# Expert weights as unsplit fp32 on 64- and 32-column tiles: experts ranked by size on chip, 1 MB chunks addressed by register

## The chip, the core and the metric

The kernel runs on one core of one Trainium2 chip. The metric is device time in microseconds (us), from the start to the end of one execution. The engines are PE (TensorE, matmuls), PEld (its weight loads), DVE (VectorE), ACT (ScalarE), POOL (GpSimd) and SP (SyncE, which here only issues transfers). All arithmetic that the reference asks for is fp32.

## What is computed

Two model blocks run one after the other on 512 tokens of width 1024. The change lies in the mixture of experts of the first block, which has 32 experts, of which each token uses four. Each expert multiplies its tokens by a 1024x2048 matrix (gate and up), applies a clipped SwiGLU, and multiplies by a 1024x1024 matrix (down).

```python
def moe_ffn(h, router_w, router_b, w_gate_up, b_gate_up, w_down, b_down):
    logits = (hf @ router_w + router_b).astype(jnp.float32)
    top_logits, top_idx = lax.top_k(logits, TOP_K)          # TOP_K = 4, N_EXPERTS = 32
    gates = jax.nn.softmax(top_logits, axis=-1)
    ...
    def expert_block(args):
        xb, e = args
        gu = xb @ w_gate_up[e] + b_gate_up[e]
        gate, up = jnp.split(gu, 2, axis=-1)
        gate = jnp.minimum(gate, SWIGLU_LIMIT)
        up = jnp.clip(up, -SWIGLU_LIMIT, SWIGLU_LIMIT)
        act = (up + 1.0) * gate * jax.nn.sigmoid(SWIGLU_ALPHA * gate)
        return act @ w_down[e] + b_down[e]
    ...
    y_sorted = yb.reshape(n_rows, d)[dest] * gate_sorted[:, None]
    out = jnp.zeros((n, d), h.dtype).at[tok_sorted].add(y_sorted)
```

Ahead of it stand a hybrid mixer and a layer norm, beside it a gated embedding (`ple`), behind it a layer norm and the second block (attention, a recurrent group and an FFN). One expert's weights are 12 MiB (12.58 MB), all 32 are 403 MB. The 512 tokens give 2048 rows, 64 for an expert on average; with the inputs that are timed the largest expert has 95.

## The kernel before

Every fp32 weight is split into two fp32r parts. `Stream` loads pieces of 128x1024 (0.5 MB) on SP's queue (L170), ACT rounds each to `hi` (L187), DVE subtracts to get `lo` (L196), and a product of 512 columns is three fp32r matmuls, `hi`x`hi`, `lo`x`hi`, `hi`x`lo` (`mm3`, L242 to L244). The tokens of an expert are the stationary operand, the weights stream past.

An expert takes up to CAP = 96 tokens, which fill 96 of the 128 columns. For expert e the loop issues `gate_up(e, 0)`, `down(e - 1)`, `gate_up(e, 1)`: two bias matmuls for each half (L976) and 144 matmuls. Between them stand the steps that prepare the expert after next: `find_a` (one-hot rows on DVE, L900), `find_b` (positions by matmul, L910), `find_c`, `gather` (POOL fetches the rows by index), and `turn` (transposes, L934, split again by ACT and DVE). `activate` is the SwiGLU on DVE and ACT, `finish` scales by the gate and POOL adds the rows into `acc` by index (L1034). What is over 96 rows goes to a loop (L1049) that runs as often as a number in `exi` says, here not at all.

The loads of SP stand in the order of use, and each waits for its place to come free: 12 raw places and some that are lent. A gate_up piece has rows of 2 KB in DRAM, a down piece rows of 4 KB. Behind the last expert `load_next` queues the first weights of block 2 (L170), the sums `rest` (L1180) and six rows of norm weights (L1176), and L1211 adds the last two experts' rows into `rest`.

Ahead of the experts stand, in this order on PE, the last of the first `ple` gate, 24 matmuls of `ple_proj`, the counts that give each row its position (L941, L944), and the second `ple` gate in four parts, with `find_b(0)` between.

Of the kernel before, what the change touches and what calls it, by code (L numbers as in the profile page):

```python
# [24 lines left out]
CAP = 96  # L25
# [13 lines left out]
    0, 128, 256, 384, 512, 544, 548, 549, 551, 583)  # L39
NC1 = 615  # L40
# [4 lines left out]
def constants():  # L45
# [5 lines left out]
    c[:, C_SLOT:C_SLOT + 128] = p[None, :]  # L51
# [30 lines left out]
def prepare(i):  # L82
# [27 lines left out]
    o["w_down"] = a["w_down"][0]  # L110
# [15 lines left out]
class Stream:  # L126
# [22 lines left out]
    def lend(self, *places):  # L149

        self.lent += places
        self.loads()

    def _load(self):
        i = self.nl
        ap, shape = self.plan[i]
        if self.lent:
            t = self.taken[i] = self.lent.pop(0)
            self.once.add(i)
        elif self.extra and i < len(self.plan) - self.keep_off:  # L160
# [12 lines left out]
    def loads(self):
        while not self.hold and self.nl < len(self.plan) and (
                self.inring < self.nring or self.lent or self.extra and self.nl < len(self.plan) - self.keep_off):
            self._load()

    def _hi(self):
        i = self.ns
        n, dest = self.units[i]  # L180
        t = self.raw[i]
        if dest is not None:
            hi, lo = dest
        else:
            hi, lo = [t_[:, :n] for t_ in self.hl(self.nh)]
            self.nh += 1
        self.nc.scalar.copy(hi, t)  # L187
        self.parts[i] = (hi, lo)
        self.half = (lo, t, hi)
        self.ns += 1  # L190

    def _lo(self):
        if self.half is not None:
            lo, t, hi = self.half
            self.half = None
            self.nc.vector.tensor_tensor(lo, t, hi, op=ALU.subtract)  # L196
            del self.raw[self.ns - 1]
            slot = self.taken.pop(self.ns - 1, None)
            if slot is None:
                self.inring -= 1  # L200
            elif self.ns - 1 not in self.once:
                self.extra.append(slot)
            self.loads()

# [18 lines left out]

@with_exitstack
def kernel(ctx: ExitStack, tc: tile.TileContext, h, out, dbg=None):
# [7 lines left out]
    psum = ctx.enter_context(tc.tile_pool(name="psum", bufs=1, space=PSUM))  # L233

# [36 lines left out]
    def raw_of(pool, n):  # L271
        return pool.tile([128, 1024], F32, tag="raw", bufs=n, name="raw")

    def parts_of(pool, n):
        return [pool.tile([128, 1024], F32R, tag=g, bufs=n, name=g) for g in ("hi", "lo")]
# [18 lines left out]
    NRING2, NHL2 = 4, 5  # L294
    st2 = Stream(nc, lambda i: raw_of(keep, 4), lambda i: parts_of(keep, 5), NRING2, NHL2)
# [8 lines left out]
    with ExitStack() as first:  # L304
        NRING, NHL = 12, 6
# [6 lines left out]
        selr = btp.tile([128, NE], F32R, name="selr")  # L312
# [3 lines left out]
        st = Stream(nc, lambda i: raw_of(keep, 4) if i % 3 == 0 else raw_of(ring, 8),  # L316
                    lambda i: parts_of(ring, 1) if i % 6 == 5 else parts_of(keep, 5), NRING, NHL)
# [47 lines left out]
        def plan_gu(e, hf):  # L365
            w = h["w_gate_up"][e].rearrange("(k p) c -> p k c", p=128)
            for k in range(2):
                for g in range(2):
                    c0 = 1024 * g + 512 * hf
                    st.add([(w[:, 4 * k:4 * k + 4, c0:c0 + 512], (4, 512))])  # L370

        def plan_d(e):
            w = h["w_down"][e].rearrange("(k p) c -> p k c", p=128)
            for k in range(4):
                st.add([(w[:, 2 * k:2 * k + 2, :], (2, D))])

        for e in range(NE):
            plan_gu(e, 0)
            if 0 < e < NE - 1:
                plan_d(e - 1)  # L380
            plan_gu(e, 1)
        plan_d(NE - 2)
        plan_d(NE - 1)
        st.keep_off = 24
# [341 lines left out]
        bts = slot("y1", [128, D])  # L726
        for r in range(4):
            c0 = 1024 * (r // 2)
            nc.sync.dma_start(bts[32 * r:32 * r + 32], h["b_gate_up"][:, c0:c0 + 1024])

        def split_biases():
            S.copy(btab, bts)
            for r in range(4):
                q = slice(32 * r, 32 * r + 32)
                S.copy(selr[q], ident[q, q])
                if r % 2:
                    tt(btab[q], bts[q], btab[q], op=ALU.subtract)
# [18 lines left out]
        st.extra.append(slot("y2", [128, D]))  # L756
        st.loads()
        ln_b(3)
        sums_start(1)
        zw2 = work.tile([128, 2, 1152], F32, tag="zw", name="zw2")  # L760
        st.extra += [zw2[:, i, 0:1024] for i in range(2)]
        st.loads()
# [3 lines left out]
        st.extra.append(slot("y3", [128, D]))  # L766
        st.loads()
# [13 lines left out]
        zz2 = new_zz((2, 1152))  # L781
        st.extra += [zz2[:, i, 0:1024] for i in range(2)]
        st.loads()
# [34 lines left out]
        M = scr[:, 128:256].rearrange("p (t e) -> p t e", t=4)  # L818
        gat = scr[:, 256:384].rearrange("p (t e) -> p t e", t=4)
        V.tensor_reduce(out=M, in_=hot4.rearrange("p t k e -> p t e k"), axis=AX.X, op=ALU.add)  # L820
        tt(hot4, hot4, ge[:, :, :, None].to_broadcast([128, 4, 4, 32]), op=ALU.mult)
        V.tensor_reduce(out=gat, in_=hot4.rearrange("p t k e -> p t e k"), axis=AX.X, op=ALU.add)
# [5 lines left out]
        V.tensor_copy(R[:, :, :, 1], gat)  # L828
        ts(posm, M, -BIG, BIG, op0=ALU.mult, op1=ALU.add)

# [34 lines left out]
        nb, ends, le = tiny[0:NE, 0:1], tiny[0:NE, 1:2], tiny[0:NE, 32:64]  # L865

        def extra_a(c):
            ts(nb, c, float(CAP), None, op0=ALU.is_gt)
            for b in range(2, 6):
                stt(nb, c, float(CAP * b), nb, op0=ALU.is_gt, op1=ALU.add)  # L870

# [6 lines left out]
        def extra_c():  # L878
# [6 lines left out]
            ts(off, off, 1.0, float(CAP), op0=ALU.add, op1=ALU.mult)  # L885
            V.tensor_copy(exi[:, XB:XB + 1], o[:, 2 * XB:2 * XB + 1])
# [7 lines left out]
        X = [None] * 2  # L894
        idx, gate, hots, onehot = {}, {}, {}, {}

        def find_a(e):
            o = zs(13 if e < 2 else 12 + e % 2, 384).rearrange("p (t s) -> p t s", t=4)
            for t in range(4):
                ts(o[:, t], cst[:, C_SLOT:C_SLOT + CAP], posm[:, t, e:e + 1], None, op0=ALU.is_equal)  # L900
            hots[e] = o

        def find_b(e, o=None, r=None):
            o = hots.pop(e) if o is None else o
            if e >= NE - 2:
                onehot[e] = o
            r = R[:, :, e] if r is None else r
# [3 lines left out]
            hots[e] = q  # L911

        def find_c(e):
            q = hots.pop(e)
            a, i = [work.tile([128, 2 - j], dt, tag=g + "n" * (e < 0), bufs=1 if e < 0 else 4, name=g)
                    for j, (g, dt) in enumerate((("ga", F32), ("ix", I32)))]
            ts(a[:CAP, 0:1], q[:CAP, 2:3], -1.0, cst[:CAP, C_NTR:C_NTR + 1], op0=ALU.add, op1=ALU.mult)
            tt(i[:CAP], a[:CAP, 0:1], q[:CAP, 0:1], op=ALU.add)
            V.tensor_copy(a[:CAP, 1:2], q[:CAP, 1:2])
            idx[e], gate[e] = i, a[:CAP, 1:2]  # L920

        def gather(e):
            x = slot(("y5" if e == 0 else "y4") if e >= 0 else "y0", [128, D])
            G.indirect_dma_start(out=x[:CAP], out_offset=None, in_=hd[:, :],
                                 in_offset=bass.IndirectOffsetOnAxis(ap=idx[e][:CAP, 0:1], axis=0))
            X[e % 2] = x

        def turn(src, dst, n=8):

            for g in range(0, n, 4):  # L930
                q = tbank()
                q3 = q.rearrange("p (c s) -> p c s", c=4)
                for c in range(4):
                    P.transpose(q3[:, c, :CAP], src[:CAP, 128 * (g + c):128 * (g + c) + 128], ident[:CAP, :CAP])  # L934
# [847 lines left out]
```

## Time and profile before

| | |
|---|---|
| median of 3 runs | 2114.42 us (2112.72 to 2117.18) |
| profiled execution | 2112.11 us, span 2110.3 us |
| mean granted PE clock | 0.993 |
| PE, DVE, ACT busy | 98%, 80%, 59% of the span |
| experts, first L976 to first L1211 | 255.2 to 1413.4 us |

Times of rows are in us from the start of the span. A row of the timeline gives the start and the length of one instruction or of a run of them; the length of a matmul is modelled to its end, so for matmuls in a row the distance between two starts is what one costs. [...]

### The profile page before, as it was taken

How to read it: one execution, taken by the hardware profiler on the slowest of the kernel's cores; microseconds unless marked ns; L12 is line 12 of the kernel's file. 1: busy time of each engine (PE TensorE's matmuls, PEld its weight loads, DVE VectorE, ACT ScalarE, POOL GpSimd, SP SyncE). 2: the span in 40 equal slices, each digit the busy share in tenths (PEclk: the TensorE clock that was granted, in tenths of full speed). 3: DMA queues.
4: the chain of work that ended last, by engine and by line, in shares of the span. 5: the costliest groups of instructions: out<-in, count | busy, mean ns of one | idle time of the engine just before them, and what ended most of it. 6: DMA issues, size and time to landing. Idle time of an engine off the chain costs nothing.

```text
span 2110.3 us, 27920 instructions
## 1 busy us (share of the span) xinstructions
PE 2066.7 (98%) x9750; PEld 1666.9 (79%) x9750; DVE 1680.6 (80%) x2372; ACT 1241.4 (59%) x1613; POOL 236.3 (11%) x118
## 2 busy tenths in 40 slices
PE   8999899999999999999999999999999899999998
PEld 7777778888888888888888888877887578888886
DVE  7967699999999999999999999996665754333454
ACT  4324377877777777777777777764234743222342
POOL 0012211212212121202111221200000000000000
PEclk9999999999999999999999999999999999999999
DMA  8236899999999999999999999773221113333321
GB/s 295 72 113 227 243 345 373 375 363 374 369 375 362 380 364 379 366 372 370 372 370 368 376 361 381 257 274 107 71 60 55 51 48 123 100 95 95 100 96 44
DMA packets 220527, 523.54 MB, mean 248 GB/s; under 512 B 17168, under 2 KB 17184, under 8 KB 220256
## 3 DMA queue, kind: packets, MB, share of 16 engines
q1 hardware_dynamic: 208352, 484.96, 64.2%
q0 software_dynamic: 10704, 35.02, 6.4%
q10 hardware_dynamic: 1328, 1.75, 0.2%
q8 instruction: 78, 1.28, 0.2%
q14 instruction: 65, 0.53, 0.1%
HBM read 500.43 MB, written 21.23 MB: 247 GB/s over the span
## 4 chain that ended last, share of the span: by engine, by line
PE 82%; DVE 3%; ACT 1%; DMA 1%; issue 1%; SPq 0%; DVEq 0%; ACTq 0%
PE mm L242 25%; PE mm L244 25%; PE mm L243 24%; PE tr L934 2%; PE mm L976 1%; PE tr L1403 1%; PE tr L910 1%; DVE lo L196 1%; PE tr L1444 0%; PE mm L1553 0%; DMA raw<-in_w_qf_dram 0%; DMA z<-in_norm_w_dram 0%; PE mm L1590 0%; PE tr L1579 0%; ACT hi L187 0%
## 5 line engine op out<-in xcount | busy, mean ns | idle before, releaser
L196 DVE TENSOR_TENSOR lo<-raw,hi 128x1024 fp32r<-128x1024 f32 (+1 forms) x565 | 665.9, 1214 | 160.9 <-ACT hi L187 156.0
L187 ACT CAST hi<-raw 128x1024 fp32r<-128x1024 f32 (+1 forms) x565 | 575.9, 1047 | 325.6 <-PE mm L243 176.0
L242 PE MATMUL mm<-hi,y 128*128 128x512 f32 x1088 | 433.5, 398 | 1.5 <-ACT y L247 1.5
L244 PE MATMUL mm<-hi,y 128*128 128x512 f32 x1088 | 425.6, 391 | 0.0
L243 PE MATMUL mm<-lo,y 128*128 128x512 f32 x1088 | 425.1, 391 | 0.0
L1034 POOL DMA_INDIRECT acc<-y,ix x30 | 177.7, 5922 | 806.6 <-DVE lo L196 780.4
L242 PEld LDWEIGHTS mm<-hi,y 128*128 128x128 f32 x1088 | 204.9, 188 | 50.6 <-issue 7.9
L244 PEld LDWEIGHTS mm<-hi,y 128*128 128x128 f32 x1088 | 204.8, 188 | 44.7 <-DVE y L248 1.3
L242 PE MATMUL mm<-hi,s 128*128 128x512 f32 x592 | 239.5, 405 | 0.0
L243 PEld LDWEIGHTS mm<-lo,y 128*128 128x128 f32 x1088 | 205.0, 188 | 40.3 <-DVE lo L196 0.4
L244 PE MATMUL mm<-hi,s 128*128 128x512 f32 x592 | 231.6, 391 | 1.4 <-DVE s L248 1.4
L243 PE MATMUL mm<-lo,s 128*128 128x512 f32 x592 | 231.3, 391 | 0.0
L196 DVE TENSOR_TENSOR lo<-s,hi 128x1024 fp32r<-128x1024 f32 x168 | 198.2, 1216 | 1.9 <-issue 1.5
L187 ACT CAST hi<-s 128x1024 fp32r<-128x1024 f32 x168 | 171.9, 1050 | 15.1 <-PE mm L244 12.3
L244 PE MATMUL mm<-vh,lo 128*128 128x512 f32 (+2 forms) x368 | 140.6, 382 | 0.1
L242 PE MATMUL mm<-vh,hi 128*128 128x512 f32 (+2 forms) x368 | 140.5, 382 | 0.0
L243 PE MATMUL mm<-vl,hi 128*128 128x512 f32 (+2 forms) x368 | 140.5, 382 | 0.0
L242 PEld LDWEIGHTS mm<-hi,s 128*128 128x128 f32 x592 | 111.5, 188 | 28.3 <-issue 7.7
L244 PEld LDWEIGHTS mm<-hi,s 128*128 128x128 f32 x592 | 111.4, 188 | 25.8 <-DVE s L248 1.8
L243 PEld LDWEIGHTS mm<-lo,s 128*128 128x128 f32 x592 | 111.7, 189 | 20.5
L1000 ACT ACTIVATE z<-z 96x512 f32<-96x512 f32 x64 | 40.5, 632 | 132.4 <-DVE z L999 132.4
L244 PEld LDWEIGHTS mm<-vh,lo 128*128 128x128 f32 x368 | 69.2, 188 | 13.6 <-DVE lo L196 0.5
(424 smaller groups left out, 3170.2 us busy)
## 6 DMA issues: line engine op xcount, KB each, us to landing
raw<-in_w_gate_up_dram SPq DMA_DIRECT2D x327, 512.0 KB, 6.8
raw<-in_w_down_dram SPq DMA_DIRECT2D x165, 512.0 KB, 7.7
s<-in_w_gate_up_dram SPq DMA_DIRECT2D x103, 512.0 KB, 8.6
s<-in_w_down_dram SPq DMA_DIRECT2D x65, 512.0 KB, 7.8
y<-in_w_gate_up_dram SPq DMA_DIRECT2D x42, 512.0 KB, 10.1
zw<-in_w_gate_up_dram SPq DMA_DIRECT2D x42, 512.0 KB, 8.3
zz<-in_w_gate_up_dram SPq DMA_DIRECT2D x42, 512.0 KB, 10.6
raw<-in_w_in_dram SPq DMA_DIRECT2D x35, 512.0 KB, 3.9
```

The costliest lines, as they stand in the source:

```text
L187: self.nc.scalar.copy(hi, t)
L196: self.nc.vector.tensor_tensor(lo, t, hi, op=ALU.subtract)
L242: P.matmul(o, a[0], b[0], start=start, stop=False)
L243: P.matmul(o, a[0], b[1], start=False, stop=False)
L244: P.matmul(o, a[1], b[0], start=False, stop=stop)
L910: P.matmul(q[:CAP, 0:3], o[:, t], r[:, t], start=(t == 0), stop=(t == 3))
L934: P.transpose(q3[:, c, :CAP], src[:CAP, 128 * (g + c):128 * (g + c) + 128], ident[:CAP, :CAP])
L976: P.matmul(o[g], selr[r, e:e + 1].to_broadcast([64, 128]), btab[r, 512 * hf:512 * hf + 512], start=True, stop=False)
L1000: act(out=s, in_=g, func=AF.Sigmoid, scale=1.702)
L1034: G.indirect_dma_start(out=acc[:, :], out_offset=bass.IndirectOffsetOnAxis(ap=idx[e][:CAP, 0:1], axis=0), in_=y[:CAP], in_offset=None, com ...
L1403: P.matmul(blk(o, b), blk(kk, b), blk(qq, b), start=True, stop=True)
```

## The change

1. The weights of the experts are no longer split. `Chunks` loads them as 128x2048 fp32 (1 MB, rows of 8 KB; `w_down` is laid out again on the host so that it has such rows too), 12 chunks for an expert, into 18 places, and the matmuls read them as they are. Each SP load waits for the eighth before it, in both kernels, so that at most eight are on their way.
2. A product of fp32 runs on a part of the columns of PE: the first 64 tokens of an expert on 64 columns (L1100, L1170), two products side by side, and for the 14 largest experts the next 32 tokens on 32 columns (L1106, L1177), four side by side, taken up once for every four chunks.
3. The experts are ranked by size on chip. The counts come from a matmul ahead of `ple_proj` (L872), DVE compares all pairs (L890 to L901), and the routing is then written in ranks. Experts 0 and 1 are always given ranks 0 and 1, so their chunks can be loaded ahead; for each of the others SP reads the expert's number from `ids` into a register (L413). The order of work mixes large and small experts.
4. The gate is applied in the SwiGLU instead of in `finish`; biases come from `pick`ed selectors; an expert's `gate_up` is done whole, and `down(i - 1)` after it.
5. Eight chunks are loaded ahead of the loop at L1049, twelve more right behind it and ahead of the first register load. The last eight chunks may only use places that block 2 doesn't need at once.

The core of the diff:

```diff
+CAP, CAPS, NL = 96, 64, 14
+class Chunks:
...
+    def loads(self):
+        while not self.hold and self.nl < min(self.limit, len(self.plan)):
+            ok = [i for i, (n, p) in enumerate(self.free) if self.nl < len(self.plan) - self.tail or n in self.last]
+            if not ok:
+                return
+            self.raw[self.nl] = place = self.free.pop(ok[0])
+            self.nc.sync.dma_start(place[1], self.plan[self.nl]())
+            self.nl += 1
...
+        def rank_a():
+            stt(key, cnt[:, 0:NE], 64.0, cst[:, C_KEY:C_KEY + NE], op0=ALU.mult, op1=ALU.add)
+            w3 = wide.rearrange("p (e f) -> p e f", e=32)
+            tt(w3, key[:, None, :].to_broadcast([128, 32, 32]), key[:, :, None].to_broadcast([128, 32, 32]), op=ALU.is_gt)
+            V.tensor_reduce(out=rank, in_=w3, axis=AX.X, op=ALU.add)
...
-        def gate_up(e, hf, pre={}, post={}):
+        def gate_up(i, pre={}, post={}):
...
-                    mm3(o[c % 2], (x[0][:, kk], x[1][:, kk]),
-                        [q[:, 512 * (k % 2):512 * (k % 2) + 512] for q in w], False, kk == 7)
+            w, n0 = [], 4 if b else 1
+            for c in range(8):
+                w.append(mo.get())
...
+                for g in range(2):
+                    for hf in range(2):
+                        c0 = 1024 * g + 512 * hf
+                        P.matmul(o[g][64 * hf:64 * hf + 64], x[:, c, 0:CAPS], w[c][:, c0:c0 + 512], start=False, stop=c == 7)
+                if (c + 1) % n0 == 0:
+                    if b:
+                        for k in range(c + 1 - n0, c + 1):
+                            for j in range(4):
+                                c0 = 1024 * (j < 2) + 512 * (j % 2)
+                                P.matmul(o[2][32 * j:32 * j + 32], x[:, k, CAPS:CAP], w[k][:, c0:c0 + 512],
+                                         start=False, stop=k == 7)
+                    mo.release(n0)
```

On PE, before the change, the beginning of a half of an expert reads as follows (`y0` and `y1` are the two parts of its tokens):

```order
L976 MATMUL mm_2719<-btab_85,selr_88 128x512
L976 MATMUL mm_2720<-btab_85,selr_88 128x512
L242 MATMUL mm_2719<-hi_2650,y0_2052 128x512
L243 MATMUL mm_2719<-lo_2651,y0_2052 128x512
L244 MATMUL mm_2719<-hi_2650,y1_2053 128x512
```

With the change a small expert has four matmuls for each chunk and nothing else in between, and a large one (the first eight rows are half of its `gate_up`) has four more of 32 rows for each chunk of a batch; `rw_99`, `zw`, `zz` and `kw_76` are places of chunks, x4 is a run of four:

```order
L1087 MATMUL mm<-btab,bs 128x512 x2
L1090 MATMUL mm<-btab,bs 128x512 x2
L1100 MATMUL mm<-rw_99,y_2790 64x512 x4
L1100 MATMUL mm<-zw_1305,y_2790 64x512 x4
L1100 MATMUL mm<-zz,y_2790 64x512 x4
L1151 MATMUL tr<-cst,z_2775 128x128 x4
L1100 MATMUL mm<-kw_76,y_2790 64x512 x4
L1106 MATMUL mm<-rw_99,y_2790 32x512 x4
L1106 MATMUL mm<-zw_1305,y_2790 32x512 x4
L1106 MATMUL mm<-zz,y_2790 32x512 x4
L1106 MATMUL mm<-kw_76,y_2790 32x512 x4
```

Gone are the three matmuls for each product, and the split parts that they waited for.

On DVE, ahead of the experts, this stood before between the top-4 choice and the first one-hot rows (`z_1510` is the one-hot of the choice, L855 adds the sums of `ple_proj`):

```order
L820 TENSOR_REDUCE z_1511<-z_1510 128x128
L821 TENSOR_TENSOR z_1510<-z_1510,z_1511 128x512
L822 TENSOR_REDUCE z_1511<-z_1510 128x128
L827 TENSOR_TENSOR y_1566<-z_1511,y_1566 128x4x32
L828 COPY R<-z_1511 128x128
L829 TENSOR_SCALAR posm<-z_1511 128x128
```

With the change the ranking stands behind the four sums of `ple_proj`, and three `lo` parts (L187) of the second `ple` gate behind the first half of the ranking:

```order
L939 TENSOR_TENSOR z_1435<-z_1435,mm 128x512
L890 SCALAR_TENSOR_TENSOR rt<-tr,cst 128x32
L892 TENSOR_TENSOR y_1461<-rt 128x1024
L893 TENSOR_REDUCE rt<-y_1461 128x32
L895 TENSOR_TENSOR y_1454<-z_1399,rt 128x512
L896 TENSOR_REDUCE rt<-y_1454 128x16
L898 TENSOR_TENSOR z_1399<-rt,cst 128x512
L900 TENSOR_REDUCE tiny<-z_1399 128x128
L901 TENSOR_SCALAR posm<-tiny 128x128
L187 TENSOR_TENSOR kh<-kw_76,kh 128x1024
```

L890 reads the counts that PE makes at L872, and PE has that matmul ahead of the 24 matmuls of `ple_proj`, not behind them.

On SP the queue right behind the loop at L1049 (now L1208) held 0.5 MB loads; now it holds the rest of the first 20 chunks, and then the first register:

```order
L231 DMA s_1942<-in_w_gate_up_dram 128x2048
L231 DMA s_1944<-in_w_gate_up_dram 128x2048
L231 DMA s_1946<-in_w_gate_up_dram 128x2048
L231 DMA s_1948<-in_w_gate_up_dram 128x2048
L231 DMA kw<-in_w_gate_up_dram 128x2048 x4
L231 DMA kw<-in_w_down_dram 128x2048
L231 DMA rw<-in_w_down_dram 128x2048
L231 DMA rw_97<-in_w_down_dram 128x2048
L231 DMA rw_98<-in_w_down_dram 128x2048
L413 TENSOR_LOAD ids
```

From there on, each chunk's load has its address from a register.

## Rows read from the trace of the kernel before

**Rows 1.** Windows by stage; us, busy of each engine, PEclk, DMA share, GB/s.

```profile
204.00:256.00 52.00, 46.42 (x223) 37.76 (x222) 31.31 (x67) 17.98 (x28) 8.24 (x12) 0.90 0.78 248
400.00:900.00 500.00, 500.00 (x2381) 404.00 (x2380) 491.40 (x597) 385.05 (x443) 100.32 (x28) 1.00 1.03 371
1392.00:1413.00 21.00, 20.23 (x95) 16.06 (x93) 20.11 (x21) 19.39 (x24) 0.00 (x0) 1.00 0.59 201
```

**Rows 2.** Instructions by source line: bias matmuls, scatters, first matmuls behind the experts.

```profile
L976 PE MATMUL mm<-btab,selr x128: 490/490/498, 255.2 to 1376.9; 64*128 64x512 f32 x128
L1034 POOL DMA_INDIRECT acc<-y,ix x30: 2396/6532/6572, 306.7 to 1354.9; - x30
L1211 PE MATMUL mm<-rest,cst x12: 590/592/697, 1413.4 to 1427.2; 128*128 128x512 f32 x12
```

**Rows 3.** Timeline of PE inside an expert (start, length, instruction).

```profile
603.01 0.83 PE L934 MATMUL tr<-cst,y 96*128 96x96 f32 x8
603.62 0.48 PE L242 MATMUL mm<-hi,s 128*128 128x512 f32 x1
...
606.25 0.39 PE L244 MATMUL mm<-hi,s 128*128 128x512 f32 x1
606.57 0.49 PE L976 MATMUL mm<-btab,selr 64*128 64x512 f32 x2
606.99 0.50 PE L242 MATMUL mm<-hi,y 128*128 128x512 f32 x1
...
611.88 0.39 PE L242 MATMUL mm<-hi,y 128*128 128x512 f32 x1
...
614.60 0.39 PE L242 MATMUL mm<-hi,y 128*128 128x512 f32 x1
```

**Rows 4.** Windows: start of the kernel, gate_up loads, down loads, indirect transfers between.

```profile
10.00:15.00 5.00, 5.00 (x21) 4.06 (x20) 4.60 (x5) 3.89 (x5) 0.00 (x0) 1.00 1.02 416
612.50:617.50 5.00, 5.00 (x26) 4.12 (x26) 5.00 (x6) 4.28 (x6) 0.00 (x0) 1.00 1.05 387
620.00:627.50 7.50, 7.50 (x35) 6.21 (x34) 7.36 (x10) 5.62 (x7) 0.00 (x0) 1.00 1.03 410
605.00:610.00 5.00, 5.00 (x23) 3.70 (x22) 4.69 (x6) 2.78 (x4) 0.04 (x1) 1.00 1.07 306
```

**Rows 5.** Timeline of PE: unsplit fp32, 64 columns (L1590) and 128 columns (L1211).

```profile
1647.40 2.37 PE L1590 MATMUL mm<-PT,va 128*64 128x512 f32 x16
1649.71 0.33 PE L1579 MATMUL tr<-cst,zz 128*128 128x128 f32 x1
...
1422.45 1.88 PE L1211 MATMUL mm<-rest,cst 128*128 128x512 f32 x4
1424.17 1.88 PE L1211 MATMUL tr<-rest,cst 128*128 128x512 f32 x4
```

**Rows 6.** The matmuls of L1590 by source line, with their forms.

```profile
L1590 PE MATMUL mm<-PT,va x16: 272/432/643, 1647.4 to 1649.5; 128*64 128x512 f32 x4, 128*64 128x384 f32 x4, 128*64 128x256 f32 x4, 128*64 128x128 f32 x4
```

**Rows 7.** Groups of DVE ahead of the experts: busy us, mean ns.

```profile
L820 DVE TENSOR_REDUCE z<-z 128x128 f32<-128x512 f32 x1 | 1.0, 1047 | 0.0
L821 DVE TENSOR_TENSOR z<-z,z 128x512 f32<-128x512 f32 x1 | 0.7, 691 | 0.0
L196 DVE TENSOR_TENSOR lo<-raw,hi 128x1024 fp32r<-128x1024 f32 x8 | 9.5, 1220 | 2.4 <-ACT hi L187 2.4
```

**Rows 8.** Timeline ahead of the experts.

```profile
209.15 1.05 DVE L820 TENSOR_REDUCE z<-z 128x128 f32<-128x512 f32 x1
...
210.35 2.39 PE L941 MATMUL tr<-z,cst 128*128 128x32 f32 x20 [0.28 <-DVE z L820]
...
246.95 0.83 SPq L170 DMA_DIRECT2D s<-in_w_down_dram  x2
```

**Rows 9.** Windows behind the loop, where PE had waited.

```profile
242.50:245.00 2.50, 0.00 (x0) 0.00 (x0) 0.00 (x0) 0.00 (x0) 0.00 (x0) 0.67 0.44 171
247.50:250.00 2.50, 2.50 (x7) 1.92 (x7) 1.00 (x2) 0.48 (x1) 0.00 (x0) 0.50 0.81 256
```

**Rows 10.** Timeline of SP behind the last expert's loads.

```profile
1391.92 16.01 SPq L170 DMA_DIRECT2D raw<-in_w_in_dram  x4
...
1412.60 3.40 SPq L1180 DMA_DIRECT2D rest<-acc  x3
```

More of the change, by code (lines that the diff above doesn't have):

```diff
@@ L269, with kh @@
     act(out=eps2, in_=eps[:, 0:1], func=AF.Sigmoid)
[L271 to L275, printed above, removed]
+    kw = [keep.tile([128, 2048], F32, name=f"kw{i}") for i in range(2)]
+    made = {}
+    def kh(i, when):
+        if (i, when) not in made:
+            made[i, when] = keep.tile([128, 2, 1024], F32R, tag=f"kh{i}", name="kh")
+        return two(made[i, when])
+    halves = lambda w: [w[:, 1024 * i:1024 * i + 1024] for i in range(2)]
+    two = lambda p: [p[:, i] for i in range(2)]
     zz = {}
@@ L363, with expert, plan_gu, plan_d @@
             st.add([(wp[:, :, 512 * n:512 * n + 512], (2, 512))])
[L365 to L373, printed above, removed]
-            for k in range(4):
[L375 to L382, printed above, removed]
-        plan_d(NE - 1)
-        st.keep_off = 24
+        place = [0, 1]
+        big, small = list(range(2, NL)), list(range(NL, NE))
+        for kind in (0, 1, 0, 1, 0) * 5 + (1, 0, 1, 0, 0):
+            place.append((big if kind else small).pop(0))
+        assert sorted(place) == list(range(NE)) and not any(r < NL for r in place[-2:])
+        reg = {}
+        def expert(i):
+            r = place[i]
+            if r < 2:
+                return ds(r, 1)
+            if r not in reg:
+                reg[r] = nc.values_load(ids[0:1, r:r + 1], engines=[ENG.SP], min_val=0, max_val=NE - 1)
+            return ds(reg[r], 1)
+        def plan_gu(i):
+            for k in range(8):
+                mo.plan.append(lambda k=k: h["w_gate_up"][expert(i), 128 * k:128 * k + 128].rearrange("a p c -> (a p) c"))
+        def plan_d(i):
+            for k in range(4):
+                mo.plan.append(lambda k=k: h["w_down"][expert(i), k].rearrange("a p c -> (a p) c"))
+        for i in range(NE):
+            plan_gu(i)
+            if i:
+                plan_d(i - 1)
+        plan_d(NE - 1)
+        mo.limit = 20
+        mo.tail, mo.last = 8, {("r", i) for i in range(4)} | {"rh", "zw", "s1", "s3"}
+        given = set()
+        def spare():
+            for n, w in whole.items():
+                a = halves(w)
+                if n not in given and all(any(x is y for y in st.free) for x in parts_[n]):
+                    given.add(n)
+                    mo.give((n, w))
+        st.done = spare
         st.loads()
@@ L922, in gather @@
[L922 to L934, printed above, removed]
-                split(dst[0][:, g:g + 4, :CAP], dst[1][:, g:g + 4, :CAP], q3[:, :, :CAP])
@@ L938 @@
+        ple_proj(0, sg0, wp0)
+        rank_a()
+        gq = tbank()
+        for t in range(4):
+            P.transpose(gq[:96, 128 * t:128 * t + 128], g3[:, t].bitcast(F32), ident)
+        og1 = [bank() for _ in range(4)]
+        ple_gate(og1, range(2))
+        rank_b()
+        gT = zs(12, 512, F32R, 96)
+        S.copy(gT, gq[:96])
+        show("gT", gT)
+        ple_sum(0, sg0, gT, [0, 1])
+        split_biases()
         pp = tbank()
@@ L1098 @@
                     if k % 4 == 0:
-                        w = load(h["w_down"], k // 4, 512 * n)
-                    P.matmul(downs[-1][n][:CAP], a32[:, k], w[:, k % 4], start=k == 0, stop=k == 7)
-            finish(-1)
-        more = slot("s3", [128, 2, D])
-        st.extra += [more[:, i] for i in range(2)]
-        st.ahead, st.hl = 4, lambda i: parts_of(keep, 5)
-        st.extra += [ring.tile([128, 1024], F32, tag=g, name="raw") for g in ("hi", "lo")]
-        st.hold = False
-        st.loads()
@@ L1131 @@
-        turn(X[0], XT[0])
+                        w = load_d(k // 4, 512 * n)
+                    P.matmul(dn[n][:CAP], a32[:, k], w[:, k % 4], start=k == 0, stop=k == 7)
+            yx = slot("s1", [128, D])
+            for n in range(2):
+                S.copy(yx[:CAP, 512 * n:512 * n + 512], dn[n][:CAP])
+            G.indirect_dma_start(out=acc[:, :], out_offset=bass.IndirectOffsetOnAxis(ap=idx[-1][:CAP, 0:1], axis=0),
+                                 in_=yx[:CAP], in_offset=None, compute_op=ALU.add)
@@ new lines @@
+        for i in range(NE):
+            pre, post = {0: [], 1: []}, {2: [], 4: [], 5: []}
+            if i > 1:
+                pre[0].append(L(finish, i - 2))
+            if i:
+                post[2].append(L(turn_act, i - 1))
+            if i + 2 < NE:
+                pre[1] += [L(find_a, i + 2), L(pick, i + 2)]
+                post[4].append(L(find_b, i + 2))
+                post[5].append(L(find_c, i + 2))
+            gate_up(i, pre, post)
+            if i == 0:
+                activate(0)
+                turn(1)
+                gather(2)
+            elif i < NE - 1:
+                down(i - 1, pre={0: [L(activate, i)]},
+                     post={1: [L(turn, i + 1)], 2: [L(gather, i + 2)] if i + 2 < NE else []})
```

503 lines of the change are left out of this document (279 added, 224 removed).

## The prediction

> **What bounds the kernel now.** I read the windows by stage first. In the steady stretch of the experts PE is busy all of the time, DVE 98% of it, and the DMA engines' share reads as full at 371 GB/s, all at full clock [rows 1]. By source line the scatters run from 306.7 to 1354.9 us in 29 steps, so an expert takes 36.14 us, and the whole stretch lasts from 255.2 to 1413.4 us [rows 2]. On the timeline of PE twelve split matmuls take 2.72 us, 0.227 each, so the 144 of an expert are 32.7 us of its 36.1 [rows 3]; the rest are biases, transposes and the search for rows. PE sets the pace. But the transfers are hardly less full. A steady window of gate_up pieces (2 KB rows) moves 387 GB/s, one of down pieces (4 KB rows) 410, and a window with the indirect gather and scatter only 306 [rows 4]. At those rates an expert's 8.39 MB of gate_up and 4.19 MB of down are 21.7 + 10.2 = 31.9 us, which leaves at most 4.2 us for the indirect rows. So whatever shortens PE's work meets the transfers soon, and the prediction is about what those can do.
>
> **PE after the change.** The trace holds unsplit fp32 on 64 columns: L1590's 16 records are two for each product, so eight products of 512, 384, 256 and 128 elements, two of each [rows 6]. They take 2.31 us to the next start [rows 5]. On 128 columns L1211's four records, two products of 512, take 1.72 us, 0.86 for one [rows 5]; eight products in a row of these lengths would be 4.3 us. So two run side by side, and a pair of 512 costs 2.31 / 2.5 = 0.92 us. A chunk has two pairs, an expert 24: 22.1 us. Around them stand biases at 0.42 us, transposes of eight at 0.61 [rows 3], and, as estimates from these, 1.9 us for transposes of the activations, the search and changes of mode (0.09 us for each of eight, from the step into the bias at 606.57 [rows 3]). A small expert is 25.0 us. A large one has 12 groups of four 32-column products; if four run side by side as two do, each is 0.92 us: 11.0 us and 2.0 us more of biases, transposes and search, 38.0 us. With 18 small and 14 large the mean is 30.7 us.
>
> No row has 32 columns; the bounds are 0.86 (a single product, mean 30.4) and 1.84 us (only two at a time, mean 35.5). I take 0.92, since the rows with 64 columns lose only 7% to a single product. [...]
>
> ACT and DVE lose 24 roundings and 24 subtractions of 1.2 us for each expert [rows 7], some 29 us of DVE's 36. Neither comes near the pace afterwards.
>
> **The transfers after the change.** All rows become 8 KB. No row of the trace has these. From 2 to 4 KB the rate went from 387 to 410, and at the start of the kernel, with nothing beside them, 4 KB rows moved 416 [rows 4]. I take 418, with 405 and 425 as bounds: 12.58 MB are 30.1 us (29.6 to 31.1). The indirect rows fall from 96 + 96 to a mean of 78 + 78, so their 4.2 us become 3.4 at most; their bytes alone, 0.8 MB at 387 GB/s, would be 2.1 and so 1.7 us. I take 3.0, near the upper end, because the share read as full. An expert is then 33.1 us of transfer (31.3 to 34.5), more than PE's 30.7: the transfers set the pace. PE waits for chunks in small experts (25 against 33) and catches up from the 18 places in large ones (38 against 33).
>
> [...]
>
> **Ahead of the experts.** What counts is when the transfers start again behind the loop: 246.95 us before [rows 8]. With 8 chunks already loaded, 376 of the 384 follow. The counts (L872) stand ahead of `ple_proj` on PE, and need the one-hot sums, which end at 209.15 + 1.05 = 210.2 [rows 8]; until then PE did the 24 matmuls of `ple_proj`, 5.4 us, which now come behind: +5.4. PE idles meanwhile, and after such a wait the granted clock was 0.67, then 0.50, in the rows behind the loop, while PE was already busy [rows 9]; some 4 us at half speed cost 2. DVE's ranking is worked out from rows of the same sizes [rows 7]: a 128x1024 compare 1.22, a reduction of it 2.1 (twice the 512-wide 1.04), two 512-wide operations at 0.69, two reductions at 1.04 and two small ones, together 7.0 us, then 3.4 us for the second half, all ahead of operations that the first expert waits for (`lo` parts of the `ple` gate, one-hot rows). DVE was busy 31.3 of 52 us in this stretch [rows 1], so part of it fits into idle time. Bounds: +7 when all of DVE's is hidden, +22 when none is and PE falls to half speed twice. I take +15: the transfers start at 262 us, PE's experts at 270. The rest of 20 chunks stands ahead of the first register load, and at 2.5 us for a chunk these cover it.
>
> **Behind the experts.** Before, SP had loads of block 2 and `rest` under way while DMA was at 0.59 in 1392 to 1413 us [rows 1], the last `rest` issued at 1412.60 [rows 10]. After it, the last chunks end just ahead of PE's last matmul, and 2.1 MB of `w_in`, 2.1 MB of `rest` and the norm rows queue behind them: about 10 us of transfer, of which I charge 5 (2 to 8), since the last down products and the sums of two experts cover the rest.
>
> **Sum.** 376 chunks are 31.33 experts: 31.33 x 33.1 = 1037 us (981 to 1081). The experts end at 262 + 1037 + 2 for the last products = 1301 instead of 1413.4: -112, +5 behind: -107. The profiled 2112.1 becomes 2004.7. The median of the runs shown is 2.3 us above it, so **2007**.
>
> **Rivals.**
> A, the forecast, with its own range 1980 to 2040 from the bounds taken singly (transfer at 34.5: +44; start at +7: -8).
> A', faster still: 425 GB/s and cheap indirect rows together, about 32 us an expert, near 1965 to 1980. For it, the 416 at the start; against it, DMA's full share in every window.
> B, PE stays the bound: 32-column groups run two at a time, large experts are 49 us, the mean 35.5. PE's experts run 270 + 32 x 35.5 = 1406, the tail is hidden: about 2105. Against it, the pairs of 64; for it, that no row shows four. A milder form, gaps that bring half speed now and then, gives 2040 to 2085.
> C, 8 KB rows are no faster than 2 KB rows: 12.58 MB at 387 are 32.5 + 3.0 = 35.5, 31.33 of them 1112, end 1376: -37 + 5, so 2082. Against it, 410 for 4 KB rows.
> D, slower: waits for chunks pull PE's clock to half. PE did run at 0.50 for a while after waits of 3 to 5 us [rows 9]; waits here are under 1 us for each chunk of a small expert. [...]
> E, slower too: a stream of larger rows that DRAM holds just under the 371 GB/s of the rows. An expert's 13.2 MB (weights and indirect rows) must come in 36.5 us for no change, which is 361 GB/s; at 355 an expert is 37.2, 31.33 of them 1165, and the time 2133. The rows speak against it: 371 held for 500 us [rows 1], and 410 without the indirect rows [rows 4]. [...]
>
> **Chances.** A 0.58, A' 0.06, B two at a time 0.08 and mild 0.08, C 0.08: faster 0.88. No change, where the ranking's delay and a PE near 36 us cancel, 0.04. D 0.07, E 0.01: slower 0.08. No change means within 0.2%, 4 us, which is what such runs can tell apart. The range runs from A' to C, 1965 to 2085, and leaves out B at two at a time, no change and slower, together 0.2.
>
> **What would show it.** Steps right: scatters 33 us apart on the mean, DMA share full at over 385 GB/s in all of the experts' stretch, PE busy some nine tenths with its waits before L1100 and L1170 put down to transfers, 64-column runs of four at 1.84 us and 32-column runs at 0.92, the last 1 MB load issued some 20 us ahead of 1300, clock at 1.00. A PE without waits and 32-column runs at 1.8 us would mean B; a rate under 395 with PE waiting, C; a granted clock well under 0.95 in the experts, D. The prediction falls if chunks land late although DMA is idle, since then the eight transfers on their way, not the rate, would set the pace.

## The result

| | before | with the change |
|---|---|---|
| median | 2113.57 us (4 runs) | 2031.28 us (4 runs, 2028.93 to 2034.2) |
| ratio to before | | 0.961, 95% interval 0.959 to 0.963 |
| span of the profiled execution | 2110.3 us | 2030.7 us |
| transfers start again behind the loop | 246.95 | 267.25 |
| PE's wait for the last chunk ends | | 1316.7 |
| first sum of the last experts | 1413.4 | 1323.4 |
| last of these sums begins | 1427.2 | 1348.0 |
| from there to the end of the span | 683.1 | 682.7 |

The forecast was 2007, with 1965 to 2085; the time fell by 82 us where 107 were forecast. The rows of the table are read from the timeline and the source lines of both kernels, and they hold the whole difference of the spans: the sums begin 90.0 us earlier, take 10.8 us longer, and the rest is the same to 0.4 us. The line of these sums in the changed kernel (before: [rows 2], L1211):

```profile
L1357 PE MATMUL mm<-rest,cst x12: 592/1061/1221, 1323.4 to 1348.0; 128*128 128x512 f32 x12
```

The page of the changed kernel shows the load of the engines (busy us, share of the span) and the chain that ended last:

```profile
PE 1906.9 (94%) x9572; PEld 1081.2 (53%) x9572; DVE 774.1 (38%) x1513; ACT 457.6 (23%) x801; POOL 100.0 (5%) x110
...
PE 46%; DMA 35%; DVE 3%; ACT 1%; issue 0%; SPq 0%; DVEq 0%; ACTq 0%
```

DMA has 35% of that chain, and DVE's load is 38% where it was 80%. The windows of the changed kernel answer to [rows 1] (us, busy of each engine, the granted clock as a share of PE's full speed, DMA share, GB/s):

```profile
204.00:256.00 52.00, 40.30 (x167) 32.87 (x166) 30.87 (x78) 10.73 (x16) 5.22 (x6) 0.77 0.38 117
500.00:600.00 100.00, 93.56 (x508) 31.86 (x508) 19.61 (x47) 9.94 (x20) 7.12 (x6) 1.00 1.02 401
600.00:700.00 100.00, 88.43 (x470) 30.16 (x468) 19.57 (x45) 9.91 (x20) 7.12 (x6) 1.00 1.02 402
1300.00:1400.00 100.00, 90.65 (x353) 57.77 (x350) 51.37 (x82) 33.61 (x60) 0.00 (x0) 0.88 0.49 178
```

In these two windows of the experts the DMA share is full at 400 GB/s and PE has gaps of 6 to 12%, at full clock. Ahead of the experts the transfers stand idle for most of the stretch (0.38) at a clock of 0.77, and behind them the clock is 0.88: these are two of the three places where the forecast had the time too small; the third is the pace of the transfers itself. What PE waited for in the experts, by the waits between 400 and 1200 us (total us, times, longest):

```profile
PE mm L1100 <- DMA kw<-in_w_gate_up_dram: 13.0, 15, 2.0
PE mm L1100 <- DMA rw<-in_w_gate_up_dram: 11.9, 13, 1.6
PE mm L1170 <- DMA kw<-in_w_down_dram: 8.0, 15, 1.4
```

Every wait in that list names a chunk, and none is over 2.0 us.

### The profile page after: what moved, and what is told of

It reads as the page before. It is cut to its first block, busy times and chain, and to the rows that moved or that the text cites. A ratio compares the mean times of both kernels' runs of the same rounds, so it can differ in the third digit from the quotient of the medians.

```text
span 2030.7 us, 24543 instructions
## 1 busy us (share of the span) xinstructions
PE 1906.9 (94%) x9572; PEld 1081.2 (53%) x9572; DVE 774.1 (38%) x1513; ACT 457.6 (23%) x801; POOL 100.0 (5%) x110
## 4 chain that ended last, share of the span: by engine, by line
PE 46%; DMA 35%; DVE 3%; ACT 1%; issue 0%; SPq 0%; DVEq 0%; ACTq 0%
PE mm L266 9%; PE mm L268 9%; PE mm L267 9%; DMA s<-in_w_gate_up_dram 8%; PE mm L1100 7%; DMA rw<-in_w_down_dram 6%; DMA kw<-in_w_down_dram 5%; DMA zw<-in_w_gate_up_dram 4%; DMA kw<-in_w_gate_up_dram 4%; DMA rw<-in_w_gate_up_dram 4%; PE mm L1170 3%; PE mm L1106 2%; PE mm L1177 1%; PE tr L1549 1%; DMA s<-in_w_down_dram 1%; DMA zz<-in_w_gate_up_dram 1%
## 5 line engine op out<-in xcount | busy, mean ns | idle before, releaser
L187 DVE TENSOR_TENSOR kh<-kw,kh 128x1024 fp32r<-128x1024 f32 (+1 forms) x116 | 139.6, 1209 | 158.0 <-ACT kh L178 157.3
L1100 PE MATMUL mm<-kw,y 128*64 128x512 f32 x768 | 180.8, 605 | 16.3 <-DMA kw<-in_w_gate_up_dram 16.1
L178 ACT CAST kh<-kw 128x1024 fp32r<-128x1024 f32 (+1 forms) x116 | 120.0, 1039 | 258.7 <-PE mm L267 170.2
L268 PE MATMUL mm<-vh,kh 128*128 128x512 f32 (+2 forms) x368 | 140.6, 382 | 0.1
L266 PE MATMUL mm<-vh,kh 128*128 128x512 f32 (+2 forms) x368 | 140.6, 382 | 0.0
L267 PE MATMUL mm<-vl,kh 128*128 128x512 f32 (+2 forms) x368 | 140.5, 382 | 0.0
L1100 PE MATMUL mm<-rw,y 128*64 128x512 f32 x512 | 121.9, 603 | 14.2 <-DMA rw<-in_w_gate_up_dram 14.2
L1100 PE MATMUL mm<-s,y 128*64 128x512 f32 x512 | 118.1, 599 | 6.7 <-DMA s<-in_w_gate_up_dram 6.4
L1100 PEld LDWEIGHTS mm<-kw,y 128*64 128x64 f32 x768 | 49.9, 137 | 115.9 <-issue 79.6
L1170 PE MATMUL mm<-kw,y 128*64 128x512 f32 x400 | 94.9, 600 | 10.4 <-DMA kw<-in_w_down_dram 10.4
L1116 DVE TENSOR_SCALAR z<-mm 128x512 f32<-128x512 f32 (+1 forms) x46 | 31.8, 692 | 166.6 <-PE mm L1100 148.7
L1170 PE MATMUL mm<-rw,y 128*64 128x512 f32 x360 | 85.8, 602 | 5.7 <-DMA rw<-in_w_down_dram 5.7
L268 PEld LDWEIGHTS mm<-vh,kh 128*128 128x128 f32 x368 | 69.1, 188 | 13.6 <-DVE kh L187 0.4
L266 PEld LDWEIGHTS mm<-vh,kh 128*128 128x128 f32 x368 | 69.2, 188 | 13.1
L267 PEld LDWEIGHTS mm<-vl,kh 128*128 128x128 f32 x368 | 69.1, 188 | 13.0
L1100 PEld LDWEIGHTS mm<-rw,y 128*64 128x64 f32 x512 | 32.0, 136 | 82.5 <-issue 53.1
L1100 PEld LDWEIGHTS mm<-s,y 128*64 128x64 f32 x512 | 33.9, 136 | 75.9 <-issue 55.5
L266 PE MATMUL mm<-kh,uh 128*128 128x512 f32 x160 | 67.7, 423 | 1.4 <-DVE ul L1408 1.2
```

The costliest lines, as they stand in the source:

```text
L266: P.matmul(o, a[0], b[0], start=start, stop=False)
L267: P.matmul(o, a[0], b[1], start=False, stop=False)
L268: P.matmul(o, a[1], b[0], start=False, stop=stop)
L1100: P.matmul(o[g][64 * hf:64 * hf + 64], x[:, c, 0:CAPS], w[c][:, c0:c0 + 512], start=False, stop=c == 7)
L1116: ts(g, pg, 7.0, None, op0=ALU.min)
L1170: P.matmul(o[0][64 * n:64 * n + 64], a[:, q, 64 * hf:64 * hf + 64], w[c][:, c0:c0 + 512], start=k == 0, stop=k == 7)
```

## The experiments

### Is it PE or the transfers?

The first run leaves out 32-column matmuls:

```diff
-                        for k in range(c + 1 - n0, c + 1):
+                        for k in range(c, c + 1) if c == 7 else ():
...
-                        for d in range(4):
+                        for d in range(3, 4):
```

> Leaves out ten of the twelve groups of 32-column matmuls of each large expert, so the output lacks most of what the rows above 64 give. Transfers set the pace (theory): the time stays within 5 us of the changed kernel's 2031. PE sets the pace (rival): 14 experts x 10 groups x 0.92 us are 129 us less, about 1902.

Measured: 2031.7 us. 140 groups of four matmuls are gone, 122 us of PE's work at the 0.87 us that the next run shows for a group, and the time stands still, so PE doesn't set the pace.

The second run leaves out the loads:

```diff
+            if self.nl < 20:
-            self.nc.sync.dma_start(place[1], self.plan[self.nl]())
+                self.nc.sync.dma_start(place[1], self.plan[self.nl]())
```

> Leaves out the loads of all chunks behind the twentieth; the matmuls read what stands in the places. Transfers set the pace: the experts then run at PE's own pace, which the terms of the sum put at 30.7 us on the mean, so 32 of them end about 1260 us instead of 1318.6, and the time is 1965 to 1975. PE sets the pace: no change. [...]

Measured: 1924.95 us, 106 less than the changed kernel and 40 to 50 less than expected. The theory holds, and PE is faster than its terms said. By source line, the weight loads of the bias matmuls in this run go from 276.3 to 1193.2 us over 31 experts, 29.6 us for each instead of 30.7:

```profile
L1088 PEld LDWEIGHTS mm<-btab,bs x64: 186/189/192, 276.3 to 1193.2; 128*128 128x128 f32 x64
```

The timeline of PE in the same run shows most of it (start, length; 16 records are eight products):

```profile
619.48 3.60 PE L1101 MATMUL mm<-s,y 128*64 128x512 f32 x16
622.91 3.60 PE L1171 MATMUL mm<-s,y 128*64 128x512 f32 x16
...
630.67 1.92 PE L1178 MATMUL mm<-s,y 128*32 128x512 f32 x16
632.41 1.90 PE L1178 MATMUL mm<-kw,y 128*32 128x512 f32 x16
```

Four pairs of 64 columns take 3.43 us to the next start, 0.86 for a pair, and two groups of four 32-column products 1.74, 0.87 for a group: two and four run side by side at the price of one product on 128 columns, 0.86 [rows 5]. Of the 40 to 50 us by which the run beats its forecast, 32 x 1.1 = 36 us come from PE's pace. The other part is the end: without chunks in the queue there is no wait for the sums, and they take 14.7 us (1224.0 to 1238.7, 592 ns for a matmul in the median) against 24.6 in the changed kernel (1061 ns).

### What sets the rate of the transfers?

The third run has no indirect rows:

```diff
+            if i > 1:
+                X[i] = X[1]
+                return
...
+            if i < 2:
-            G.indirect_dma_start(out=acc[:, :], out_offset=bass.IndirectOffsetOnAxis(ap=idx[i][:n, 0:1], axis=0),
+                G.indirect_dma_start(out=acc[:, :], out_offset=bass.IndirectOffsetOnAxis(ap=idx[i][:n, 0:1], axis=0),
```

> Leaves out the gathers of all experts but the first two and all scatters but two (every expert reads the rows of the second, and what the others compute is not added up). Indirect rows cost the transfers 3.8 us for each expert (theory: 33.5 measured less 29.7 at the 423 GB/s of clean windows): transfers fall to 29.7, PE's 30.7 to 31 take over, 2.5 to 2.8 us less for each expert, 80 to 88 us in all, about 1947. They cost only their bytes, 1.7 us (rival, the remainder being gaps between chunks): about 53 us less, 1978.

Measured: 1940.32 us, 7 under the lower of the two. The window of this run, and the weight loads of its bias matmuls:

```profile
400.00:900.00 500.00, 500.00 (x2774) 179.29 (x2772) 115.78 (x259) 57.42 (x113) 0.00 (x0) 1.00 1.01 421
...
L1090 PEld LDWEIGHTS mm<-btab,bs x64: 186/189/192, 275.2 to 1192.2; 128*128 128x128 f32 x64
```

Chunks of 8 KB rows alone move 421 GB/s, and PE has no gap: both limits, 29.9 us for an expert's 12.58 MB and PE's 29.6, now lie beside each other. PE takes 917 us for 31 experts, as in the run without loads, so the 91 us that this run gains are cut short by PE, and the transfers alone could be a little faster than 421. In the changed kernel 376 chunks, 394.3 MB, took 1316.7 - 267.25 = 1049.4 us. At 421 they would be 936; the remainder of 113 us is 3.6 for each expert, the figure that the next two runs were forecast from. The windows of the changed kernel show what indirect rows do to the rate:

```profile
632.50:635.00 2.50, 2.13 (x10) 0.48 (x8) 0.95 (x2) 0.33 (x1) 0.00 (x0) 1.00 1.01 426
...
645.00:647.50 2.50, 2.50 (x28) 0.78 (x24) 0.00 (x0) 0.89 (x2) 0.00 (x0) 1.00 1.01 316
```

The second lies 4 to 7 us behind the gather that POOL issued at 640.58 us.

Two runs leave out one kind each, with the upper or the lower part of the diff above:

> Leaves out the scatters of 28 experts, whose rows are then not added up; the gathers stay. All indirect rows cost the transfers 3.6 us an expert (1049 us of transfers less the 936 that 394 MB take at 421 GB/s, over 31.33). If scatters cost more than gathers since they read and write the sums (theory), some 2.4 us: 28 of them 67 us, but the wait for the sums stays, about 1964. If both cost the same (rival), 1.8 us: 50 us, about 1981.

> Leaves out the gathers of all experts but the first two (each later one reads the second's rows); the scatters stay. Theory: the remainder of the 3.6 us, 1.2 us for each of 30, 36 us, about 1995. Rival (the same cost): 54 us, about 1977.

Measured: 1992.13 without 28 scatters, 39 us less, 1.4 each; 1980.57 without 30 gathers, 51 us less, 1.7 each. The theory that scatters cost more fell: the gathers cost a little more.

Together that is 3.1 and not 3.6. The bytes of SP's queue, which carries nothing but chunks between 400 and 900 us, settle it:

| | chunks in 500 us | for an expert's 12.58 MB |
|---|---|---|
| changed kernel | 188.80 MB | 33.3 us |
| without scatters | 197.61 MB | 31.8 us |
| without gathers | 199.98 MB | 31.5 us |
| without either | 209.84 MB | 30.0 us |

Scatters cost 1.5 us an expert there, gathers 1.9, both 3.3, so they add up. At 33.3 the 376 chunks would take 1044 us; some 5 of the 1049.4 belong to the beginning, where the queue moved only 9.62 MB of chunks up to 300 us.

Two runs keep everything but the length of a row in DRAM, here the one of 2 KB (the other has halves instead of quarters):

```diff
+    w = a["w_gate_up"][0].reshape(NE, 8, 128, 4, 512).transpose(0, 1, 3, 2, 4)
+    o["w_gate_up"] = np.ascontiguousarray(w)
...
-            self.nc.sync.dma_start(place[1], self.plan[self.nl]())
+            self.nc.sync.dma_start(place[1].rearrange("p (j c) -> p j c", j=4), self.plan[self.nl]())
```

> The same 1 MB chunks in the same places, but laid out in DRAM with rows of 2 KB instead of 8 KB. The length of a row sets the rate (theory): 387 GB/s as in the windows of 2 KB rows before, 32.5 + 3.8 = 36.3 us for an expert instead of 33.5, 31.33 of them 88 us more, about 2119. The rate of before came from elsewhere (0.5 MB transfers, or PE's pace; rival): within 10 us of 2031.

> The same 1 MB chunks laid out in DRAM with rows of 4 KB. The length of a row sets the rate (theory): 410 GB/s as in the windows of 4 KB rows before, 30.7 us an expert against 29.9 at the 421 of 8 KB rows, 31.33 of them 25 us more than 2031, about 2056. Only rows as short as 2 KB cost anything (rival): within 6 us of 2031.

Measured: 2105.98 and 2052.25 us, 75 and 21 above the changed kernel. Windows of the run with 2 KB rows, then of the one with 4 KB rows:

```profile
400.00:900.00 500.00, 436.20 (x2312) 146.43 (x2312) 94.29 (x212) 48.07 (x96) 34.67 (x29) 0.99 1.05 373
...
607.50:610.00 2.50, 2.50 (x16) 0.95 (x14) 0.46 (x1) 0.00 (x0) 0.00 (x0) 1.00 1.05 384
```

```profile
400.00:900.00 500.00, 460.93 (x2466) 157.74 (x2462) 102.33 (x230) 50.23 (x99) 36.62 (x31) 0.99 1.03 391
602.50:612.50 10.00, 10.00 (x64) 2.93 (x62) 4.89 (x7) 1.26 (x2) 0.00 (x0) 1.00 1.02 408
```

The forecasts were 2119 and 2056, so the theory holds in both, with a little less lost than it said. 384, 408 and 421 GB/s where nothing indirect runs, and 387 and 410 for 2 and 4 KB rows before [rows 4]: over these rows the rate goes with the length of the row, with transfers of 1 MB as with those of 0.5 MB. With 2 KB rows the changed kernel would be only 0.4% faster than the one before (ratio 0.996, 0.9946 to 0.9974).

One run asks for the size of the transfer itself:

```diff
-            self.nc.sync.dma_start(place[1], self.plan[self.nl]())
+            src = self.plan[self.nl]()
+            for q in range(2):
+                self.nc.sync.dma_start(place[1][64 * q:64 * q + 64], src[64 * q:64 * q + 64])
```

> Each 1 MB chunk is loaded by two transfers of 64 partitions and 0.5 MB, with the rows of 8 KB kept; eight transfers on their way are then 4 MB, as before the change. The length of a row sets the rate, not the size of a transfer (theory): within 8 us of 2031. The size counts too (rival): the rate falls to the 410 of 0.5 MB transfers with 4 KB rows or under, 2050 or more.

Measured: 2581.29 us. Its four times lie between 2533 and 2673, too far apart for a ratio, but all are 500 us and more above the changed kernel. The window of the run:

```profile
900.00:1400.00 500.00, 358.12 (x1680) 117.77 (x1680) 67.56 (x152) 36.19 (x72) 26.13 (x22) 0.91 1.02 280
```

Neither forecast has a time like this, nor a DMA share that reads as full at 280 GB/s. The run changed two things at once, the bytes of a transfer and the partitions that it covers. Since 0.5 MB over 128 partitions moved 387 and 410 before [rows 4], the 64 partitions are the likelier cause, which no run here tells apart.

### The two ends

Behind the experts, the changed kernel's timeline and windows show where the extra 10.8 us went:

```profile
1323.36 2.05 PE L1357 MATMUL mm<-rest,cst 128*128 128x512 f32 x2 [4.72 <-DMA rest<-acc]
```

```profile
1320.00:1324.00 4.00, 0.64 (x1) 0.50 (x2) 3.72 (x4) 3.10 (x4) 0.00 (x0) 0.62 0.88 311
1324.00:1328.00 4.00, 4.00 (x6) 1.00 (x4) 1.70 (x3) 0.58 (x1) 0.00 (x0) 0.50 1.01 348
...
1340.00:1344.00 4.00, 4.00 (x7) 1.92 (x7) 0.30 (x1) 0.01 (x1) 0.00 (x0) 0.50 0.29 76
```

PE waits 4.72 us for the first sum, which queued behind the last chunks and 2.1 MB of block 2's weights; then the clock is 0.50 until 1344 us, though PE is busy all the time, and a matmul of the sums takes up to 1221 ns, where the shortest takes 592. If that one wait brings the half clock, both go with it: 4.7 us, and the 10 us by which the sums take longer than in the run without loads (24.6 against 14.7), 15 together, about 2016. One run changes the order there:

```diff
-            st2.loads()
             load_sums(0)
+            load_sums(1)
+            st2.loads()
             load_rows()
...
-             post={1: [ahead], 2: [ahead], 3: [ahead, ahead, ahead]})
+             post={})
         ys.append(finish_parts(NE - 1))
+        for _ in range(5):
+            ahead()
```

> Behind the last expert, the loads of the sums' first two tiles stand ahead of block 2's first weights in SP's queue, and ACT rounds those weights behind the last expert's rows instead of ahead of them. [...] PE falls to half speed anyway, from the waits for the last chunks (rival): only the wait goes, about 2026.

Measured: 2020.26 us, 11 less by the medians, and 2016.8 against 2030.7 for the spans of the profiled executions, 14 less; the 15 of the one wait are nearer than the rival's 5. The wait is gone, the sums take 1315.9 to 1330.6 (first row), and the clock stays at 1.00 in this run's windows (last two rows):

```profile
L1360 PE MATMUL mm<-rest,cst x12: 592/592/697, 1315.9 to 1330.6; 128*128 128x512 f32 x12
...
1314.07 1.94 PE L1170 MATMUL mm<-s,y 128*64 128x512 f32 x8 [0.57 <-DMA s<-in_w_down_dram]
...
1320.00:1324.00 4.00, 4.00 (x19) 3.27 (x18) 3.75 (x4) 2.42 (x3) 0.00 (x0) 1.00 0.91 324
1324.00:1328.00 4.00, 4.00 (x14) 2.19 (x14) 3.45 (x8) 0.29 (x1) 0.00 (x0) 1.00 1.01 388
```

So without the one wait of 4.7 us there is no half clock in these windows; the waits of about half a us for the last chunks, which stayed (the second row), don't bring it.

Ahead of the experts, the changed kernel's timeline has two waits of PE and the restart of the transfers:

```profile
212.42 1.89 PE L872 MATMUL tr<-tiny,cst 128*128 128x32 f32 x8 [5.65 <-DVE tiny L870]
...
233.46 1.22 PE L944 MATMUL mm<-y,z 96*128 96x512 f32 x2 [5.67 <-ACT z L1051]
...
267.25 2.54 SPq L231 DMA_DIRECT2D s<-in_w_gate_up_dram  x4
```

The first is the wait for the one-hot sums that the forecast named. The second it did not: the gate table's copy (L1051) goes into the buffer that held the top-4 values, which DVE reads at L904, behind all of the first half of the ranking and three `lo` parts. DVE's first and last step of that half, L904, and the wait of the copy for it (total us, times, longest):

```profile
222.50 0.18 DVE L890 SCALAR_TENSOR_TENSOR rt<-tr,cst 128x32 f32<-128x32 f32 x1
...
228.49 0.23 DVE L901 TENSOR_SCALAR posm<-tiny 128x128 f32<-128x128 f32 x1
...
232.04 0.68 DVE L904 TENSOR_TENSOR y<-z,z 128x512 f32<-128x512 f32 x1
...
ACT z L1051 <- DVE y L904: 15.5, 1, 15.5
```

One run moves both:

```diff
         ple_proj(0, sg0, wp0)
+        for t in range(4):
+            P.matmul(cnt[:, 0:NE], ones, M[:, t], start=t == 0, stop=t == 3)
         rank_a()
...
         extra_a(pp[0:NE, 128:129])
+        rank_b()
+        find_a(0)
         ple_gate(og1, [2, 3])
+        P.matmul(pp[0:1, 132:164], cst[0:NE, C_TOK:C_TOK + 1], perm[0:NE], start=True, stop=True)
+        V.tensor_copy(ids, pp[0:1, 132:164])
+        gT = zs(12, 512, F32R, 96)
+        S.copy(gT, gq[:96])
```

> Ahead of the experts, the counts stand behind the 24 matmuls of the first projection instead of ahead of them, and the second half of the ranking, the gate table's sums and the experts' numbers stand behind the positions. PE's two waits of 5.7 us and the half speed behind them delay the start of the transfers (theory): transfers start 10 to 18 us earlier than 267, and since they set the pace the time falls by as much, 2013 to 2021. The start is set elsewhere, by DVE's chain, which is as long as before (rival): under 4 us.

Measured: 2021.18 us, 10 less by the medians, just outside the forecast's 2013 to 2021; transfers start at 253.83, 13.4 us earlier, and the spans of the profiled executions differ by 14.4. The first sum begins 14.1 us earlier, so what the start gains, the end gains:

```profile
253.83 2.95 SPq L231 DMA_DIRECT2D s<-in_w_gate_up_dram  x4
...
L1357 PE MATMUL mm<-rest,cst x12: 592/958/1221, 1309.3 to 1333.5; 128*128 128x512 f32 x12
```

The two together, with two places given ahead of the loop:

```diff
+        for i in (0, 2):
+            mo.give((f"s{i}", slot(f"s{i}", [128, 2048])))
         ple_gate(og1, [4, 5])
```

> Both of these, and two of the places given to chunks ahead of the loop, where the transfers idle, instead of behind it. Theory: two chunks more ahead are 5 us, so 15 + 14 + 5 = 34 us less than 2031, about 1997. If the places only come free when the transfers start anyway (rival for the third part), about 2002.

Measured: 2004.94 us, ratio to before 0.9481 (0.9465 to 0.9497), the fastest version of the study. The first sum starts at 1303.4, against 1309.3 with the wait of 4.7 in the run before: by these rows the two chunks ahead brought about 1 us, not 5. The medians don't tell it apart: 26 us together against 11 and 10 singly, in executions that lie 5 to 7 us apart. A window right behind the loop, in the run before (without the two chunks) and in this one:

```profile
260.00:268.00 8.00, 8.00 (x38) 4.82 (x38) 5.27 (x11) 0.30 (x1) 4.39 (x5) 1.00 1.03 348
```

```profile
260.00:268.00 8.00, 8.00 (x37) 4.97 (x37) 5.49 (x11) 0.30 (x1) 4.39 (x5) 1.00 0.76 158
```

The transfers that had gone ahead left a hole, since the next places come free only behind the loop. The last run gives those earlier too:

```diff
+        ple_end(1, sg1, gT)
+        mo.give(*[(f"kh{i}", keep.tile([128, 2048], F32, tag=f"kh{i}", name="kw")) for i in range(5)],
+                ("rh", ring.tile([128, 2048], F32, tag="rh", name="rw")))
         st.hold = mo.hold = True
```

> The combined version, in which two chunks moved ahead gained 1 us instead of 5, since the transfers then idled until the six places of the split weights came free behind the loop. Here the second projection stands ahead of the loop, and its places are given there. If the places were the limit (theory), the transfers run on from 258 us instead of 264, and the time is 4 to 8 us under the combined version's 2005, about 1999. If the loop's own wait is what holds them (rival), the same or slower.

Measured: 2023.79 us, 19 above the combined version. The waits of PE in that run name the place:

```profile
PE tr L1140 <- SPq L1213: 24.8, 1, 24.8
...
268.00:276.00 8.00, 0.00 (x0) 0.00 (x0) 0.00 (x0) 0.00 (x0) 0.00 (x0) 0.50 1.04 377
276.00:284.00 8.00, 0.00 (x0) 0.00 (x0) 0.00 (x0) 0.00 (x0) 0.00 (x0) 0.50 0.61 258
```

L1213 is the loop that runs no time here. SP reached it behind its loads, whose issue ended at 264.6. From 268 to 284 no engine did anything while the six chunks came in, and PE went on at 284.85. The rival holds: the loads under way at the loop delayed all engines, PE by 24.8 us.

## Why the prediction was right, and where it was off

**What sets the pace.** Right: without most of the 32-column matmuls the time is the same, without the loads it falls by 106 us, and PE's waits name chunks. Rival B is out (0.87 us for a group of four, against 1.84), and so is a limit under 371 GB/s (E), since 400 were sustained with the indirect rows in them. Rival C is out: 421 against 387. A' had the rate nearly right, but the indirect rows are not cheap.

**PE's term** was 30.7 us for an expert and measured 29.6, because a pair is 0.86 instead of 0.92 and a group 0.87. These alone would take off 1.7, so the rest around them costs some 0.6 more than the estimates. It changes nothing in the sum. The bound of a single product was the truth: 0.87 for a group of four, 0.86 for one [rows 5].

**The transfers' term** was 33.1 us and measured 1049.4 / 31.33 = 33.5: +12 us. Its two parts were off in opposite ways. The rate was 421 instead of 418. The indirect rows cost 3.3 in the middle of the stretch instead of 3.0; the upper bound of 3.4 was nearer. With them an expert is 33.3 there, which is 7 of the 12 us. The other 5 are the slow beginning of the stretch, which the forecast put at nothing; what slows it, no run here separates. The runs settle what the forecast left open, that 8 KB rows do better: 421 against the 408 of the run with 4 KB rows.

**The start** was +15 and measured +20.3, within its bounds. The ranking itself took 6.2 us on DVE for the first half, less than the 7.0 of the sum, since its 1024-wide reduction was 1.22 and not 2.1; what was missed is the second wait of 5.67 us, through a shared buffer, which the order of the instructions alone doesn't show. The clock was charged from [rows 9], where only the second window has PE busy at 0.50; in the first, at 0.67, PE is idle.

**The end** was +5, taken from the middle of 2 to 8, and measured 4.7 for the wait, and then 10.8 for sums at half clock. This last is the term that was left out: the rows on the clock [rows 9] were used ahead of the experts and not behind them. It is what rival D names, a half clock after a wait, at another place than D had it: in the experts no wait was over 2.0 us, and the clock stayed at 0.98 to 1.00 in windows of 100 us.

These add up: 5.3 + 12.4 + 10.8, less 0.7 for the small ones, is 27.8, which is 107.4 forecast less 79.6 measured for the spans. All the large ones go the same way, so the time isn't near the forecast by luck of two errors against each other.

**What the gain hangs on.** Splitting disappeared from DVE and ACT, as forecast, and was worth little by itself: with rows of 2 KB the unsplit kernel, with its later start and longer end, gains 0.4%. About 75 of its 82 us hang on the rows of 8 KB, which came with the 1 MB chunks. That unsplit matmuls were needed to use them is argued from PE's 36.1 us an expert before; no run gives the old kernel such rows.

## What to carry to other kernels

When PE and the transfers are both near full, price both after the change, and give the transfers' rate by the length of a row in DRAM (here 384, 408 and 421 GB/s for 2, 4 and 8 KB). Where transfers set the pace, look at what stands ahead of the first of them, and at shared buffers there: in one run a start 13.4 us earlier brought the sums at the end 14.1 us earlier. Here a wait of 4.7 us cost another 10.8, since matmuls followed it at a clock of 0.50; let what they wait for go ahead in the queue. And don't take a remainder (1049 less 936) for the price of one cause before a run has taken that cause out.

## What the runs showed that was not expected

- Four fp32 products of 32 columns took 0.87 us, the same as one of 128 columns (0.86).
- After one wait of 4.7 us the granted clock stayed at 0.50 for some 20 us of busy PE; after the waits ahead of the experts it came back within 6 to 12 us.
- Gathers of 64 to 96 rows cost the transfers 1.9 us each in the middle of the stretch, scatters that add 1.5.
- With transfers of 64 partitions, 0.5 MB and 8 KB rows, a window of 500 us moved 280 GB/s at a DMA share of 1.02.
- A loop that runs no time held all engines while loads were on their way, PE for 24.8 us.
- A reduction of 128x1024 along its row took 1.22 us; the 512-wide one of before, whose terms lie 32 elements apart, took 1.04 [rows 7].
